# Two matmuls of 512 and 256 columns in place of three of 256 in a split-float32 network

## Chip, cores and metric

One Trainium2 chip, one core, one launch. The metric is the device time of the launch in microseconds (us); the time before is 1345.1 us, the median of three runs. A smaller time is better.

## What is computed

The reference takes 256 tokens of 1024 features through two blocks.

- Block 1: an RMS norm, one wide projection, sliding-window attention with 8 heads, chunkwise retention with 4 heads, two sigmoid gates that merge them, an output projection, and a SwiGLU feed-forward layer of 2816 hidden units.
- Block 2: a gated spatial mixer beside a banded attention, an output projection, and a PEER layer: a query projection per token, scores against two sets of 128 keys for each of 8 heads, a top-16 of the 16 x 16 sums of the best, and then, over the chosen ones of 16384 experts, `sum over experts of softmax(score) * gelu(u . x) * v`.

```python
u = jnp.take(expert_u, eidx, axis=0)
h = jax.nn.gelu(jnp.einsum('thkd,td->thk', u, xb))
vv = jnp.take(expert_v, eidx, axis=0)
return jnp.einsum('thk,thkd->td', (g * h.astype(jnp.float32)).astype(xb.dtype), vv)
```

The kernel computes the products with all experts densely and then multiplies by a matrix S of gates that is zero where an expert was not chosen.

## The kernel before

**Split products.** Every large product runs in `fp32r` with both factors split into a high and a low part, x = xh + xl and W = Wh + Wl, and keeps three of the four partial products. `mm3` (L105 to L109) issues them for one chunk of 128 along the contracted axis: Wh with xh (L107), Wh with xl (L108), Wl with xh (L109). The weights are the stationary operand (128 x 128), the activations stream with 256 columns, one per token, and all three add into the same 256 columns of a PSUM bank. `new_acts` (L206) keeps xh and xl in two tiles, `acth` and `actl` (also `hidh`, `atth`, `xbh`).

**Weights.** `unit_` (L80 to L97) loads a unit of up to 8 such chunks (512 KB) by one DMA on SP's queue into `raw` (4 buffers); ScalarE (ACT) copies it to `whi` (L94) and VectorE (DVE) subtracts to `wlo` (L95). The parts live in two pools of three buffers in the two blocks (`wa`, `wb`, taken in turn) and in `wb` alone in the PEER layer. A unit is asked for with a priority that lies 80 ahead (`AHEAD`), and the compiler's scheduler fixes from the priorities one order of instructions for each engine; every engine then works through its own in order.

**PSUM.** Eight banks of 512 columns: four named `mm`, handed out by `mm_bank` (L99) for these products, and four named `ax` (L102) for the rest.

**Who reads the banks.** A tile of 256 columns is read once, by the instruction that also uses it: the first projections by DVE with the norm's factor R (L286), the gates by DVE (L324), the att/ret pairs by DVE (L341, L342), `w_out`, `w_down` and `w_out2` by a DVE add of the residual (L357, L402, L645), the gated half of block 2 by DVE (L589), the queries by ACT (L898). In the feed-forward layer (gate and up) and in PEER's first layer (`first_layer`, L921) two units fill the two halves of one bank, which is read with 512 columns at once: DVE L383, and ACT's Gelu L933, L936.

**Order of the PEER layer.** Six queries with activations before the norm (`RAWQ`), then 128 units `peer_u`; among the first of them the other ten queries are laid in (after every third unit), with their score matmuls (L837), and DVE's top-k steps are handed out by a budget (`pump`). When those are done, two or three calls of `combine` (L851: four tokens each, DVE and ACT build one-hot matrices, 8 small matmuls) follow each pair of units. After that come 128 units `peer_v`, the second layer (L974), with 512 columns. `gemm_n` (L136), which makes some projections with the weights streaming in 512 columns, and the second layer use four or more banks directly.

Of the kernel before, what the change touches and what calls it, by code (L numbers as in the profile page):

```python
# [13 lines left out]
OP = mybir.AluOpType  # L14
# [28 lines left out]
class Net:  # L43
    def __init__(self, tc, a, out, stack):
        self.tc, self.nc, self.a, self.out, self.stack = tc, tc.nc, a, out, stack
        nc = self.nc
        self.const = self.pool("const", 1)
        self.psum = self.pool("psum", 1, space=PSUM)
        self.tiny = self.pool("tiny", 2)
        self.small = self.const.tile([128, NSMALL], F32, name="small")  # L50
# [47 lines left out]

    def mm_bank(self):  # L99
        return self.psum.tile([128, 512], F32, name="mm", bufs=4)  # L100
# [21 lines left out]
    def gemm_k(self, ps, parts, hl, ks, first=False, last=False):  # L122
        hi, lo = parts
        for k in ks:
            s = slice(k * 128, k * 128 + 128)
            self.mm3(ps, (hi[:, s], lo[:, s]), self.acts(hl, k), first and k == ks[0], last and k == ks[-1])

    def gemm_t_late(self, jobs, hl):
        """gemm_t of several (ps, src), with the last k after all others."""
# [6 lines left out]
    def gemm_n(self, src, hl):  # L136
        """two banks, one per 128 tokens, of [t, 512] for a chunk of 512 columns."""
# [19 lines left out]
    def rsqrt(self, y, ss, n, scale, pool=None):  # L157
        """y = (ss * scale + eps)^-1/2, all [128, n]."""
# [22 lines left out]
    def token_sums(self, acc):  # L181
        """[128 t, 2] from [128 d, 256 t] summed over d."""
# [6 lines left out]
    def rows(self, r, name):  # L189
        """[128, 256] with r of token t in column t, in every partition."""  # L190
# [40 lines left out]
    def block1(self, actp):  # L231
        nc, a, tc = self.nc, self.a, self.tc
        mult, add, sub = OP.mult, OP.add, OP.subtract
        with ExitStack():
# [19 lines left out]
            with ExitStack() as s1:  # L254
# [12 lines left out]
                for i, (dst, sc) in enumerate(dests):  # L267
                    ps = (self.ax_bank() if i in (3, 4) else self.mm_bank())[:, :T]
# [4 lines left out]
                    early.append((dst, sc, ps))  # L273
# [11 lines left out]
                    for d_, c_, p_ in early:  # L285
                        nc.vector.scalar_tensor_tensor(d_, p_, c_, R, op0=mult, op1=mult)  # L286
# [34 lines left out]
                for i in range(16):  # L321
                    ps = self.mm_bank()[:, :T]
                    self.gemm_t(ps, a["w_in_a"][14 + i], h, 8)
                    nc.vector.tensor_tensor(out=gate[:, i], in0=ps, in1=R, op=mult)  # L324
                    if i == 2:
                        self.turn_ret(osb, ret)
                    if i % 4 == 3:
                        g4 = gate[:, i - 3:i + 1].rearrange("p a b -> p (a b)")
                        nc.scalar.activation(g4, g4, AF.Sigmoid)
                mer = self.new_acts(actp)  # L330
                for m in range(8):
                    if m % 2 == 0:
                        hi, lo = self.unit(a["w_att_o"][m // 2], 1024)
                    ps = self.mm_bank()
                    for k in range(4):
                        s = slice((m % 2 * 4 + k) * 128, (m % 2 * 4 + k) * 128 + 128)
                        self.mm3(ps[:, :T], (hi[:, s], lo[:, s]), self.acts(att, k), k == 0, k == 3)
                    self.gemm_t(ps[:, T:], a["w_ret_o"][m], ret, 8)
                    m1 = p2.tile([128, T], F32, name="m1")
                    m2 = p2.tile([128, T], F32, name="m2")  # L340
                    nc.vector.tensor_tensor(out=m1, in0=ps[:, :T], in1=gate[:, m], op=mult)  # L341
                    nc.vector.tensor_tensor(out=m2, in0=ps[:, T:], in1=gate[:, 8 + m], op=mult)  # L342
                    nc.vector.tensor_tensor(out=m1, in0=m1, in1=m2, op=add)
# [4 lines left out]
                for m in range(8):  # L348
                    if m == 0:
                        two = [self.mm_bank()[:, :T] for _ in range(2)]  # L350
# [3 lines left out]
                    else:  # L354
                        ps = self.mm_bank()[:, :T]
                        self.gemm_t(ps, a["w_out"][m], mer, 8)
                    nc.vector.tensor_tensor(out=x1[:, m], in0=ps, in1=x0[:, m], op=add)  # L357
                    self.split(x1[:, m], h[0][:, m], h[1][:, m], self.col("norm_ffn", m))
                    self.accumulate_squares(acc, x1[:, m], m)
            with ExitStack() as s1:  # L360
# [4 lines left out]
                for f in range(KF):  # L365
                    ps = self.mm_bank()
                    if f == 0:
                        other = self.mm_bank()
                        self.gemm_t_late([(ps[:, :T], a["w_gate"][0]), (other[:, :T], a["w_up"][0])], h)
                        r = self.norm_column(acc, "rb")  # L370
                        early.append((ps[:, :T], other[:, :T]))
                        continue
                    self.gemm_t(ps[:, :T], a["w_gate"][f], h, 8)
                    if f == 2:
                        R = self.rows(r, "rb")
                    self.gemm_t(ps[:, T:], a["w_up"][f], h, 8)
                    early.append((ps.rearrange("p (a t) -> p a t", a=2), None))
                    if f == 1:
                        continue
                    for f0, (g, u) in enumerate(early, f + 1 - len(early)):  # L380
                        gu = p2.tile([128, 2, T], F32, name="gu")
                        if f0:
                            nc.vector.tensor_tensor(out=gu, in0=g, in1=R[:, None, :].to_broadcast([128, 2, T]),  # L383
                                                    op=mult)
                        else:
                            nc.vector.tensor_tensor(out=gu[:, 0], in0=g, in1=R, op=mult)
                            nc.vector.tensor_tensor(out=gu[:, 1], in0=u, in1=R, op=mult)
# [10 lines left out]
                for m in range(8):  # L398
                    ps = self.mm_bank()[:, :T]
# [114 lines left out]
    def block2(self, actp, x2, h, acc, acg):  # L514
        nc, a = self.nc, self.a
        mult, add, sub = OP.mult, OP.add, OP.subtract
        with ExitStack() as s1:
# [68 lines left out]
            def gated(m):  # L586
                ps = self.mm_bank()[:, :T]
                self.gemm_t(ps, a["w_in2_a"][m], h, 8)
                nc.vector.tensor_tensor(out=u[:, m], in0=ps, in1=R, op=mult)  # L589
# [30 lines left out]
            def begin(m):  # L620
                outs.append((self.mm_bank()[:, :T], self.unit(a["w_out2"][m], 1024)))
# [15 lines left out]
            for m in range(8):  # L637
# [4 lines left out]
                else:  # L642
                    ps = self.mm_bank()[:, :T]
                    self.gemm_t(ps, a["w_out2"][m], ab, 8)
                nc.vector.tensor_tensor(out=x3[:, m], in0=ps, in1=y, op=add)  # L645
# [56 lines left out]
    def peer(self, st, x3, h, acc):  # L702
# [181 lines left out]
        def query(c):  # L884
            nonlocal last, keys, r, R
            if c == 0:
                firsts[:] = [self.mm_bank()[:, :T] for _ in range(2)]
# [3 lines left out]
            else:  # L891
                ps = self.mm_bank()[:, :T]
# [5 lines left out]
            nc.scalar.activation(qT, ps, AF.Copy)  # L898
# [22 lines left out]
        def first_layer(j):  # L921
            nonlocal pair
            e = j % 2
            if e == 0:
                pair = self.mm_bank()
            self.gemm_t(pair[:, e * T:e * T + T], a["peer_u"][j], xb, 8)
# [3 lines left out]
            p3 = pair.rearrange("p (e t) -> p e t", e=2)  # L930
            if done:
                gt = cp.tile([128, 2, T], F32, name="gt", bufs=2)
                nc.scalar.activation(gt[:, :, :done], p3[:, :, :done], AF.Gelu_apprx_tanh)  # L933
                nc.vector.tensor_tensor(out=S[:, js, :done], in0=S[:, js, :done], in1=gt[:, :, :done], op=mult)
            if done < T:
                nc.scalar.activation(S[:, js, done:], p3[:, :, done:], AF.Gelu_apprx_tanh)  # L936
# [64 lines left out]
def wt(w, ks=None):  # L1001
    """[n chunk][128 k][k chunk * 128 n]"""
# [4 lines left out]
def wn(w):  # L1007
    """[n chunk of 512][pair of k chunks][128 k][2 * 512 n]"""
# [77 lines left out]
```

## Time and profile before

| | |
|---|---|
| three runs | 1344.84, 1345.1, 1346.21 us |
| profiled execution: span from first to last instruction | 1343.6 us |
| TensorE matmul (PE) busy | 1334.3 us, 99% |
| weight loads (PEld) busy, beside the matmuls | 1245.0 us, 93% |
| DVE busy | 935.0 us, 70% |
| ACT busy | 768.4 us, 57% |
| mean granted TensorE clock | 0.997 of full |

The profiled execution has no time of its own beside its span; the median is 1.5 us above that span. Durations below are from this execution. Matmuls overlap, so a matmul's own duration (some 0.28 us) says little; the interval from one start to the next says what it costs. "Issue interval" below means that interval.

### The profile page before, as it was taken

The numbers are of one execution on the slowest core, as the hardware profiler recorded it, in microseconds if no ns is written. First come the engines' busy times: TensorE is split into PE (matmuls) and PEld (weight loads), VectorE is DVE, ScalarE is ACT, GpSimd is POOL, SyncE is SP. The second block draws the span as 40 slices with busy tenths as digits, with TensorE's granted clock in tenths as the row PEclk, the third lists the DMA queues.
The fourth block names the chain that finished last, engine by engine and source line by source line (L and its number), as shares of the span: only waits on it lengthen the run. The fifth ranks groups of instructions, "written<-read, shape, count | busy, mean of one in ns | idle before, by whom it ended". The sixth has DMA issues, their size and how long they took to land.

```text
span 1343.6 us, 24086 instructions
## 1 busy us (share of the span) xinstructions
PE 1334.3 (99%) x9384; PEld 1245.0 (93%) x9384; DVE 935.0 (70%) x1826; ACT 768.4 (57%) x1306; POOL 9.7 (1%) x12
## 2 busy tenths in 40 slices
PE   8999999999999999999999999999999999999998
PEld 8878999999998899999999999999998888888887
DVE  6767576766666977966996667777656666665665
ACT  5456445544455766444458887776555555555553
POOL 2000000000000000000000000000000000000000
PEclk8999999999999999999999999999999999999999
DMA  8545666666566446656564444444576666666664
GB/s 267 179 137 159 187 179 185 186 189 181 176 192 228 142 138 181 191 180 184 151 197 147 142 141 137 140 137 139 157 219 190 192 198 191 194 195 191 196 194 126
DMA packets 67633, 236.27 MB, mean 176 GB/s; under 512 B 7616, under 2 KB 9536, under 8 KB 67392
## 3 DMA queue, kind: packets, MB, share of 16 engines
q1 hardware_dynamic: 66512, 233.14, 57.1%
q8 instruction: 73, 1.20, 0.4%
q10 hardware_dynamic: 1008, 1.61, 0.3%
q14 instruction: 40, 0.33, 0.1%
HBM read 232.62 MB, written 2.10 MB: 175 GB/s over the span
## 4 chain that ended last, share of the span: by engine, by line
PE 95%; DVE 2%; DMA 1%; issue 0%; ACT 0%; POOL 0%; SPq 0%; ACTq 0%; POOLq 0%; DVEq 0%
PE ax L974 26%; PE mm L107 21%; PE mm L109 21%; PE mm L108 21%; PE ax L872 5%; DVE wlo L95 1%; DMA raw<-in_w_in_a_dram 1%; PE ax L837 0%; DMA xT<-in_xT_dram 0%; ACT whi L94 0%; PE ax L663 0%; PE ax L698 0%; PE ax L464 0%; PE ax L452 0%; PE ax L685 0%
## 5 line engine op out<-in xcount | busy, mean ns | idle before, releaser
L95 DVE TENSOR_TENSOR wlo<-raw,whi 128x1024 fp32r<-128x1024 f32 (+2 forms) x433 | 524.5, 1213 | 225.9 <-ACT whi L94 224.8
L94 ACT ACTIVATE whi<-raw 128x1024 fp32r<-128x1024 f32 (+3 forms) x439 | 458.0, 1046 | 332.9 <-PE mm L108 249.0
L107 PE MATMUL mm<-xbh,whi 128*128 128x256 f32 x1104 | 316.2, 287 | 0.0
L109 PE MATMUL mm<-xbh,wlo 128*128 128x256 f32 x1104 | 312.4, 283 | 0.8 <-DVE wlo L95 0.7
L108 PE MATMUL mm<-xbl,whi 128*128 128x256 f32 x1104 | 312.1, 283 | 0.0
L107 PE MATMUL mm<-acth,whi 128*128 128x256 f32 x848 | 241.0, 284 | 1.7 <-ACT acth L248 1.0
L108 PE MATMUL mm<-actl,whi 128*128 128x256 f32 x848 | 239.7, 283 | 0.7 <-DVE actl L249 0.7
L109 PE MATMUL mm<-acth,wlo 128*128 128x256 f32 x848 | 239.6, 283 | 0.0
L109 PEld LDWEIGHTS mm<-xbh,wlo 128*128 128x128 f32 x1104 | 210.6, 191 | 1.3 <-DVE wlo L95 1.2
L107 PEld LDWEIGHTS mm<-xbh,whi 128*128 128x128 f32 x1104 | 211.2, 191 | 0.2
L108 PEld LDWEIGHTS mm<-xbl,whi 128*128 128x128 f32 x1104 | 210.8, 191 | 0.0
L107 PEld LDWEIGHTS mm<-acth,whi 128*128 128x128 f32 x848 | 161.3, 190 | 2.8 <-ACT acth L248 1.2
L108 PEld LDWEIGHTS mm<-actl,whi 128*128 128x128 f32 x848 | 161.2, 190 | 1.6 <-DVE actl L249 1.6
L109 PEld LDWEIGHTS mm<-acth,wlo 128*128 128x128 f32 x848 | 161.3, 190 | 0.2 <-DVE wlo L95 0.2
L974 PE MATMUL ax<-wlo,keys 128*128 128x512 f32 x512 | 158.0, 389 | 0.0
L974 PE MATMUL ax<-whi,q 128*128 128x512 f32 x512 | 158.0, 389 | 0.0
L974 PE MATMUL ax<-whi,keys 128*128 128x512 f32 x512 | 157.9, 389 | 0.0
L151 ACT ACTIVATE keys<-S 128x256 fp32r<-128x256 f32 x128 | 53.4, 418 | 151.5 <-PE ax L974 151.5
L974 PEld LDWEIGHTS ax<-whi,q 128*128 128x128 f32 x512 | 96.1, 188 | 20.0
L974 PEld LDWEIGHTS ax<-wlo,keys 128*128 128x128 f32 x512 | 96.1, 188 | 19.9
L974 PEld LDWEIGHTS ax<-whi,keys 128*128 128x128 f32 x512 | 96.1, 188 | 19.8
L865 ACT ACTIVATE G<-B,ga 128x128 f16<-128x128 f16 x256 | 98.0, 575 | 0.0
(277 smaller groups left out, 1468.7 us busy)
## 6 DMA issues: line engine op xcount, KB each, us to landing
raw<-in_peer_u_dram SPq DMA_DIRECT2D x128, 512.0 KB, 3.6
raw<-in_peer_v_dram SPq DMA_DIRECT2D x128, 512.0 KB, 4.2
raw<-in_w_in_b_dram SPq DMA_DIRECT2D x32, 512.0 KB, 4.3
raw<-in_w_in_a_dram SPq DMA_DIRECT2D x31, 512.0 KB, 3.9
raw<-in_w_gate_dram SPq DMA_DIRECT2D x22, 512.0 KB, 3.6
raw<-in_w_up_dram SPq DMA_DIRECT2D x22, 512.0 KB, 3.7
raw<-in_w_out_dram SPq DMA_DIRECT2D x16, 512.0 KB, 4.3
raw<-in_w_down_dram SPq DMA_DIRECT2D x16, 512.0 KB, 3.6
```

The costliest lines, as they stand in the source:

```text
L94: self.last_copy = nc.scalar.activation(hi[:, s], raw[:, s], AF.Copy).ins
L95: (engine or nc.vector).tensor_tensor(out=lo[:, s], in0=raw[:, s], in1=hi[:, s].bitcast(F32), op=OP.subtract)
L107: mm(ps, lhsT=left[0], rhs=right[0], start=first, stop=False)
L108: mm(ps, lhsT=left[0], rhs=right[1], start=False, stop=False)
L109: mm(ps, lhsT=left[1], rhs=right[0], start=False, stop=last)
L151: nc.scalar.activation(hi, src, AF.Copy)
L865: nc.scalar.activation(G[0][:, :, t], B[:, :, t], AF.Copy, scale=ga[:, t0 + t:t0 + t + 1])
L872: nc.tensor.matmul(C[:, t * 128:t * 128 + 128], lhsT=A[:, :, t], rhs=G[i][:, :, t], start=i == 0, stop=i == 1)
L974: nc.tensor.matmul(banks[tb][d], lhsT=s[left][:, ts], rhs=w[right][:, d * 512:d * 512 + 512], start=first, stop=end)
```

## The change

The activations' two parts become two halves of one tile of 512 columns for each chunk. A new `wide` issues one matmul of Wh with all 512 columns, into a whole bank (xh's product in the first half, xl's in the second), and one of Wl with xh's 256 columns into the first half. So one weight load and one matmul in three go, and the columns streamed stay the same (768). The bank's halves are added when it is read: `total` does it with an ACT copy of the second half to SBUF and a DVE add of the first; `plus` with two DVE adds.

A tile of 256 results now takes a whole bank. `mm_pair` makes tiles of two banks, two buffers; `mm_bank` hands out first one half of such a pair, then the other. What was one bank for two units (feed-forward, att/ret, first layer) is a pair. What used the bank on reading (the factor R, the gate, Gelu) now follows from SBUF as an instruction of its own. `gemm_n` and the second layer keep their matmuls. Docstrings were taken out.

```diff
+    def mm_pair(self):
+        return self.psum.tile([128, 2, 512], F32, name="mm", bufs=2)
     def mm_bank(self):
-        return self.psum.tile([128, 512], F32, name="mm", bufs=4)
+        if self.half is None:
+            self.half = self.mm_pair()
+            return self.half[:, 0]
+        pair, self.half = self.half, None
+        return pair[:, 1]
...
+    def wide(self, ps, w, hl, k, first, last):
+        mm = self.nc.tensor.matmul
+        mm(ps, lhsT=w[0], rhs=hl[2][:, k].rearrange("p h t -> p (h t)"), start=first, stop=False)
+        mm(ps[:, :T], lhsT=w[1], rhs=hl[0][:, k], start=False, stop=last)
+    def total(self, out, ps):
+        self.nc.scalar.activation(out, ps[..., T:], AF.Copy)
+        self.nc.vector.tensor_tensor(out=out, in0=ps[..., :T], in1=out, op=OP.add)
+    def plus(self, out, x, ps):
+        tt = self.nc.vector.tensor_tensor
+        tt(out=out, in0=ps[:, :T], in1=x, op=OP.add)
+        tt(out=out, in0=ps[:, T:], in1=out, op=OP.add)
...
-            self.mm3(ps, (hi[:, s], lo[:, s]), self.acts(hl, k0 + k),
-                     first and k == 0, last and k == K - 1)
+            self.wide(ps, (hi[:, s], lo[:, s]), hl, k0 + k, first and k == 0, last and k == K - 1)
...
     def new_acts(self, pool, K=8, tag="act", bufs=2):
-        return (pool.tile([128, K, T], F32R, tag=tag + "h", name=tag + "h", bufs=bufs),
-                pool.tile([128, K, T], F32R, tag=tag + "l", name=tag + "l", bufs=bufs))
+        both = pool.tile([128, K, 2, T], F32R, tag=tag, name=tag, bufs=bufs)
+        return both[:, :, 0], both[:, :, 1], both
...
-                    ps = self.mm_bank()[:, :T]
+                    ps = self.mm_bank()
                     self.gemm_t(ps, a["w_in_a"][14 + i], h, 8)
-                    nc.vector.tensor_tensor(out=gate[:, i], in0=ps, in1=R, op=mult)
+                    self.total(gate[:, i], ps)
...
-                        g4 = gate[:, i - 3:i + 1].rearrange("p a b -> p (a b)")
+                        g4 = gate[:, i - 3:i + 1]
+                        nc.vector.tensor_tensor(out=g4, in0=g4, in1=R[:, None, :].to_broadcast([128, 4, T]), op=mult)
                         nc.scalar.activation(g4, g4, AF.Sigmoid)
...
-                    nc.vector.tensor_tensor(out=x2[:, m], in0=ps, in1=x1[:, m], op=add)
+                    self.plus(x2[:, m], x1[:, m], ps)
...
-            nc.scalar.activation(qT, ps, AF.Copy)
+            self.total(qT, ps)
...
             if e == 0:
-                pair = self.mm_bank()
-            self.gemm_t(pair[:, e * T:e * T + T], a["peer_u"][j], xb, 8)
+                pair = self.mm_pair()
+            self.gemm_t(pair[:, e], a["peer_u"][j], xb, 8)
...
             if done:
                 gt = cp.tile([128, 2, T], F32, name="gt", bufs=2)
-                nc.scalar.activation(gt[:, :, :done], p3[:, :, :done], AF.Gelu_apprx_tanh)
+                self.total(gt, pair)
+                nc.scalar.activation(gt[:, :, :done], gt[:, :, :done], AF.Gelu_apprx_tanh)
                 nc.vector.tensor_tensor(out=S[:, js, :done], in0=S[:, js, :done], in1=gt[:, :, :done], op=mult)
+            else:
+                gt = S[:, js]
+                self.total(gt, pair)
             if done < T:
-                nc.scalar.activation(S[:, js, done:], p3[:, :, done:], AF.Gelu_apprx_tanh)
+                nc.scalar.activation(S[:, js, done:], gt[:, :, done:], AF.Gelu_apprx_tanh)
```

The scheduler's new order, at three places. In the changed kernel `unit_`'s two lines are L95 and L96, `wide` is L125 and L126, `total` L129 and L130, `plus` L135 and L136. A row is one instruction: line, operation, output and inputs with tile numbers, shape, and the semaphores it waits on (`DVE_49` counts DVE's instructions, `Activation_49` ACT's, `PE_49` TensorE's).

First place, TensorE in `w_down`, at the change from one output tile to the next (`hid` is the hidden activations, `whi` and `wlo` the unit's parts, `mm` the bank). Before:

```order
L107 MATMUL mm_4171<-hidh_2474,whi_4233 128x256
L108 MATMUL mm_4171<-hidl_2475,whi_4233 128x256
L109 MATMUL mm_4171<-hidh_2474,wlo_4234 128x256
L107 MATMUL mm_4265<-hidh_2474,whi_4267 128x256 [waits Activation_49]
L108 MATMUL mm_4265<-hidl_2475,whi_4267 128x256
L109 MATMUL mm_4265<-hidh_2474,wlo_4268 128x256 [waits DVE_49]
```

Now:

```order
L126 MATMUL mm_3444<-hid_2102,wlo_3491 128x256
L125 MATMUL mm_3589<-hid_2102,whi_3591 128x512 [waits DVE_49,Activation_49]
L126 MATMUL mm_3589<-hid_2102,wlo_3592 128x256 [waits DVE_49]
L125 MATMUL mm_3589<-hid_2102,whi_3591 128x512
L126 MATMUL mm_3589<-hid_2102,wlo_3592 128x256
L125 MATMUL mm_3589<-hid_2102,whi_3591 128x512
L126 MATMUL mm_3589<-hid_2102,wlo_3592 128x256
L125 MATMUL mm_3589<-hid_2102,whi_3591 128x512
L125 MATMUL mm_3444<-hid_2102,whi_3518 128x512 [waits DVE_49]
L126 MATMUL mm_3444<-hid_2102,wlo_3519 128x256
```

Before, the next tile (`mm_4265`) follows at once and its two waits are for its weights. Now the first tile of pair `mm_3444` ends, seven matmuls of another pair follow, and the first matmul of the second half of `mm_3444` waits for DVE's two adds (L135, L136) that read its first half.

Second place, TensorE in the PEER layer where queries are laid in (`xb` the normed activations, L861 the score matmuls, `qT` a query read from its bank, `mm_5288` and `mm_5311` two pairs of the two buffers, `mm_5387` the pair that takes the buffer of `mm_5288`):

```order
L125 MATMUL mm_5288<-xb_4915,whi_5356 128x512
L126 MATMUL mm_5288<-xb_4915,wlo_5357 128x256
L861 MATMUL ax_5467<-keys_5334,qT_5336 128x128 [waits DMAHW5_49,DVE_49]
L861 MATMUL ax_5467<-keys_5334,qT_5336 128x128
L125 MATMUL mm_5311<-xb_4915,whi_5443 128x512 [waits Activation_49]
L126 MATMUL mm_5311<-xb_4915,wlo_5444 128x256 [waits DVE_49]
L125 MATMUL mm_5311<-xb_4915,whi_5443 128x512
L126 MATMUL mm_5311<-xb_4915,wlo_5444 128x256
L125 MATMUL mm_5311<-xb_4915,whi_5443 128x512
L125 MATMUL mm_5387<-xb_4915,whi_5389 128x512 [waits DVE_49]
L126 MATMUL mm_5387<-xb_4915,wlo_5390 128x256
```

The last matmul of `mm_5288` is followed by two score matmuls and five of `mm_5311`; then `mm_5387` waits until DVE has read `mm_5288`.

Third place, DVE among the gates of block 1 (`gate<-mm` at L130 is the add of `total`):

```order
L96 TENSOR_TENSOR wlo_1431<-raw_1429,whi_1430 128x1024 [waits DMAHW0_49,PE_49,Activation_49]
L130 TENSOR_TENSOR gate_1091<-mm_1228,gate_1091 128x256 [waits Activation_49]
L96 TENSOR_TENSOR wlo_1404<-raw_1402,whi_1403 128x1024 [waits DMAHW7_49,Activation_49]
L130 TENSOR_TENSOR gate_1091<-mm_1277,gate_1091 128x256 [waits Activation_49]
L96 TENSOR_TENSOR wlo_1455<-raw_1453,whi_1454 128x1024 [waits DMAHW1_49,PE_49,Activation_49]
L130 TENSOR_TENSOR gate_1091<-mm_1277,gate_1091 128x256 [waits Activation_49]
```

Each add that reads a bank now stands behind a weight subtraction (`wlo`) which itself waits for ACT's `whi` and for TensorE to have done with an earlier unit.

## Rows read from the trace of the kernel before

**Rows 1.** Page, part 1 (busy time, share, instructions) and the granted clock by slices.

```profile
PE 1334.3 (99%) x9384; PEld 1245.0 (93%) x9384; DVE 935.0 (70%) x1826; ACT 768.4 (57%) x1306; POOL 9.7 (1%) x12
...
PEclk8999999999999999999999999999999999999999
```

**Rows 2.** Page, part 4, the chain that ended last, by engine and line.

```profile
PE 95%; DVE 2%; DMA 1%; issue 0%; ACT 0%; POOL 0%; SPq 0%; ACTq 0%; POOLq 0%; DVEq 0%
PE ax L974 26%; PE mm L107 21%; PE mm L109 21%; PE mm L108 21%; PE ax L872 5%; DVE wlo L95 1%; DMA raw<-in_w_in_a_dram 1%; PE ax L837 0%; DMA xT<-in_xT_dram 0%; ACT whi L94 0%; PE ax L663 0%; PE ax L698 0%; PE ax L464 0%; PE ax L452 0%; PE ax L685 0%
```

**Rows 3.** Groups by form, L107: tile and inputs, shape, count | busy us, mean ns.

```profile
L107 PE MATMUL mm<-xbh,whi 128*128 128x256 f32 x1104 | 316.2, 287 | 0.0
...
L107 PE MATMUL mm<-acth,whi 128*128 128x256 f32 x848 | 241.0, 284 | 1.7 <-ACT acth L248 1.0 <-DVE aq L286 0.7
...
L107 PE MATMUL mm<-hidh,whi 128*128 128x256 f32 x176 | 49.4, 281 | 0.0
```

**Rows 4.** PE timeline, 256 columns: PEER layer, then gates (start, duration; 18 and 33 intervals).

```profile
699.74 0.28 PE L107 MATMUL mm<-xbh,whi 128*128 128x256 f32 x1
...
701.90 0.28 PE L107 MATMUL mm<-xbh,whi 128*128 128x256 f32 x1
...
148.01 0.28 PE L107 MATMUL mm<-acth,whi 128*128 128x256 f32 x1
...
151.92 0.28 PE L107 MATMUL mm<-acth,whi 128*128 128x256 f32 x1
```

**Rows 5.** 512 columns: chain's row of the second layer; PE timeline of `gemm_n` (23 intervals).

```profile
991.45 347.52 PE ax L974 x1533
...
106.46 0.39 PE L108 MATMUL mm<-wlo,acth 128*128 128x512 f32 x1
...
111.83 0.39 PE L107 MATMUL mm<-whi,acth 128*128 128x512 f32 x1
```

**Rows 6.** PE, ACT and DVE timelines where one gate's unit ends at 150.50.

```profile
150.50 0.28 PE L107 MATMUL mm<-acth,whi 128*128 128x256 f32 x1
...
150.63 1.06 ACT L94 ACTIVATE whi<-raw 128x1024 fp32r<-128x1024 f32 x1 [1.78 <-PE mm L108]
...
150.70 0.42 DVE L324 TENSOR_TENSOR gate<-mm,ra 128x256 f32<-128x256 f32 x1 [0.60 <-PE mm L109]
151.72 1.23 DVE L95 TENSOR_TENSOR wlo<-raw,whi 128x1024 fp32r<-128x1024 f32 x1 [0.60 <-ACT whi L94]
```

**Rows 7.** DVE timeline in the combine stage, where an instruction follows `wlo` without a gap.

```profile
782.86 1.22 DVE L95 TENSOR_TENSOR wlo<-raw,whi 128x1024 fp32r<-128x1024 f32 x1
783.99 0.80 DVE L875 SCALAR_TENSOR_TENSOR S<-ax,S 128x280 f32<-128x280 f32 x2
```

**Rows 8.** Groups by form: reads of a bank by ACT and DVE; one-hot copies of `combine`.

```profile
L898 ACT ACTIVATE qT<-mm 128x256 f32<-128x256 f32 x16 | 5.9, 368 | 0.4 <-ACT xt L918 0.4
...
L936 ACT ACTIVATE S<-mm 128x512 f32<-128x512 f32 x26 | 15.1, 580 | 0.0
...
L383 DVE TENSOR_TENSOR gu<-mm,rb 128x512 f32<-128x512 f32 x21 | 14.5, 691 | 9.4 <-PE mm L109 9.3
...
L865 ACT ACTIVATE G<-B,ga 128x128 f16<-128x128 f16 x256 | 98.0, 575 | 0.0
```

**Rows 9.** Windows: length; busy us (instructions) of PE, PEld, DVE, ACT, POOL; clock, DMA share, GB/s.

```profile
654.00:699.00 45.00, 44.23 (x365) 43.69 (x364) 44.53 (x111) 22.98 (x29) 0.00 (x0) 1.00 0.54 159
705.00:958.00 253.00, 253.00 (x2119) 250.76 (x2118) 182.48 (x353) 192.30 (x453) 0.00 (x0) 1.00 0.47 141
```

**Rows 10.** DVE timeline of 654 to 699 (first and last `wlo`, 14 intervals), and PE's wait there.

```profile
654.09 1.21 DVE L95 TENSOR_TENSOR wlo<-raw,whi 128x1024 fp32r<-128x1024 f32 x1
...
698.64 2.35 DVE L95 TENSOR_TENSOR wlo<-raw,whi 128x1024 fp32r<-128x1024 f32 x2
...
PE mm L109 <- DVE wlo L95: 0.7, 1, 0.7
```

More of the change, by code (lines that the diff above doesn't have):

```diff
@@ L125, in gemm_k @@
             s = slice(k * 128, k * 128 + 128)
-            self.mm3(ps, (hi[:, s], lo[:, s]), self.acts(hl, k), first and k == ks[0], last and k == ks[-1])
+            self.wide(ps, (hi[:, s], lo[:, s]), hl, k, first and k == ks[0], last and k == ks[-1])
     def gemm_t_late(self, jobs, hl):
@@ L272, in block1 @@
                     self.gemm_t(ps, a["w_in_a"][i], h, 8, parts=parts, engine=nc.gpsimd if i in (4, 5) else None)
-                    early.append((dst, sc, ps))
+                    self.total(dst, ps)
+                    early.append((dst, sc))
                     if i == 1:
@@ L284, in block1 @@
                         R = self.rows(r, "ra")
[L285 to L286 removed]
+                    for d_, c_ in early:
+                        nc.vector.scalar_tensor_tensor(d_, d_, c_, R, op0=mult, op1=mult)
                     early = []
@@ L333, in block1 @@
                         hi, lo = self.unit(a["w_att_o"][m // 2], 1024)
-                    ps = self.mm_bank()
+                    ps = self.mm_pair()
                     for k in range(4):
                         s = slice((m % 2 * 4 + k) * 128, (m % 2 * 4 + k) * 128 + 128)
[L337 to L343, printed above, removed]
+                        self.wide(ps[:, 0], (hi[:, s], lo[:, s]), att, k, k == 0, k == 3)
+                    self.gemm_t(ps[:, 1], a["w_ret_o"][m], ret, 8)
+                    mm = p2.tile([128, 2, T], F32, name="mm")
+                    self.total(mm, ps)
+                    nc.vector.tensor_tensor(out=mm, in0=mm, in1=gate[:, m:m + 9:8], op=mult)
+                    m1 = mm[:, 0]
+                    nc.vector.tensor_tensor(out=m1, in0=m1, in1=mm[:, 1], op=add)
                     self.split(m1, mer[0][:, m], mer[1][:, m])
@@ L349, in block1 @@
                     if m == 0:
-                        two = [self.mm_bank()[:, :T] for _ in range(2)]
+                        two = [self.mm_bank() for _ in range(2)]
                         self.gemm_t_late(list(zip(two, a["w_out"][0:2])), mer)
@@ L354, in block1 @@
                     else:
-                        ps = self.mm_bank()[:, :T]
+                        ps = self.mm_bank()
                         self.gemm_t(ps, a["w_out"][m], mer, 8)
-                    nc.vector.tensor_tensor(out=x1[:, m], in0=ps, in1=x0[:, m], op=add)
+                    self.plus(x1[:, m], x0[:, m], ps)
                     self.split(x1[:, m], h[0][:, m], h[1][:, m], self.col("norm_ffn", m))
@@ L365, in block1 @@
                 for f in range(KF):
-                    ps = self.mm_bank()
+                    ps = self.mm_pair()
                     if f == 0:
-                        other = self.mm_bank()
-                        self.gemm_t_late([(ps[:, :T], a["w_gate"][0]), (other[:, :T], a["w_up"][0])], h)
+                        self.gemm_t_late([(ps[:, 0], a["w_gate"][0]), (ps[:, 1], a["w_up"][0])], h)
                         r = self.norm_column(acc, "rb")
-                        early.append((ps[:, :T], other[:, :T]))
-                        continue
[L373 to L387, printed above, removed]
+                    else:
+                        self.gemm_t(ps[:, 0], a["w_gate"][f], h, 8)
+                        if f == 2:
+                            R = self.rows(r, "rb")
+                        self.gemm_t(ps[:, 1], a["w_up"][f], h, 8)
+                    gu = p2.tile([128, 2, T], F32, name="gu", bufs=3)
+                    self.total(gu, ps)
+                    early.append((f, gu))
+                    if f < 2:
+                        continue
+                    for f0, gu in early:
+                        nc.vector.tensor_tensor(out=gu, in0=gu, in1=R[:, None, :].to_broadcast([128, 2, T]), op=mult)
                         nc.scalar.activation(gu[:, 0], gu[:, 0], AF.Silu)
@@ L642, in block2 @@
                 else:
-                    ps = self.mm_bank()[:, :T]
+                    ps = self.mm_bank()
                     self.gemm_t(ps, a["w_out2"][m], ab, 8)
-                nc.vector.tensor_tensor(out=x3[:, m], in0=ps, in1=y, op=add)
+                self.plus(x3[:, m], y, ps)
                 self.split(x3[:, m], h[0][:, m], h[1][:, m], self.col("ln_ffn", m))
@@ L886, in query @@
             if c == 0:
-                firsts[:] = [self.mm_bank()[:, :T] for _ in range(2)]
+                firsts[:] = [self.mm_bank() for _ in range(2)]
                 self.gemm_t_late(list(zip(firsts, a["w_q"][0:2])), h)
```

16 lines of the change are left out of this document (9 added, 7 removed).

## The prediction
> **What bounds the kernel now.** I read the busy times first: TensorE works 99% of the span, weight loads run beside it for 93%, VectorE (DVE) has 30% and ScalarE (ACT) 43% of the time free [rows 1]. The granted clock is at its full level, 2.4 GHz, in all slices but the first. The chain of waits agrees: 95% of it is TensorE, three times 21% of that the lines of `mm3` [rows 2]. So whatever shortens TensorE's own work shows in the time, and whatever makes TensorE wait shows as well. For other engines' work one asks only whether something waits for it.
>
> Then what a matmul costs. In the PEER layer 18 issue intervals of 256-column matmuls take 701.90 - 699.74 = 2.16 us, 120.0 ns each; among the gates 33 take 3.91 us, 118.5 ns [rows 4]. In the second layer 1533 matmuls of 512 columns take 347.52 us, 226.7 ns each; in `gemm_n` 23 intervals take 5.37 us, 233.5 ns [rows 5]. From 256 to 512 columns the price rises by 106.7 ns, not by 120: some 13 ns of a matmul with its weight load don't depend on the columns. Those 13 ns are what the change can save, once for each three.
>
> **Term 1, the dropped matmul.** A triple costs 360.0 ns in the PEER layer and would cost 226.7 + 120.0 = 346.7, a gain of 13.3; with 1104 triples there [rows 3] this is 14.7 us. In the blocks it is 355.5 against 226.7 + 118.5 = 345.2, a gain of 10.3; with 848 + 176 triples 10.5 us. Together **-25.2 us**. That is the good end as rows show it, since every row of either width pays for its load. At the other end the wide matmul costs what it does in `gemm_n`, 233.5: gains of 6.5 and 3.5 ns, so 7.2 + 3.6 = 10.8 us. I take 25.2, because the second layer's matmuls come in the same setting (PEER layer, weights from the same pool) and are by far the larger sample.
>
> **Term 2, reading the halves: added work on ACT and DVE.** A read of 256 columns costs ACT 368 ns and a read of 512 costs 580; DVE takes 691 for 512 [rows 8] and 0.42 us for 256 [rows 6]. Each tile or pair gains one ACT copy and one DVE instruction of that size, where one read was enough. As busy time I cost this at nothing, because ACT and DVE are 57% and 70% busy; the cover goes where DVE has no time left, which is term 4. What matters first is when the read is over, for the bank is free only then.
>
> **Term 3, the wait for a bank.** Before, four `mm` banks go round one by one, and waits for a bank's reader are all but absent (0.7 us behind L286 in the row of the 848 [rows 3]): a gate's unit ends at 150.50, and DVE reads it at 150.70, done at 151.12, 0.6 us after the end [rows 6]. DVE can do so since ACT makes the next `whi` meanwhile (150.63, 1.06 us), and `wlo` comes after (151.72).
>
> Now the read needs both engines in turn, and the order puts weights ahead of it on both. After the unit's end `whi` starts 0.13 later; 1.09 after that `wlo`; the next DVE instruction starts 1.13 after `wlo` [rows 7]; the add takes 0.42. The read ends **0.13 + 1.09 + 1.13 + 0.42 = 2.77 us after the unit's end**, call it the latency L. With `whi` alone ahead (0.13 + 1.06 + 0.37 + 0.42) it is near 1.95; with nothing ahead (0.13 + 0.37 + 0.06 + 0.42) near 1.0. Pairs and `plus` add 0.3.
>
> Whether TensorE waits depends on the work it has between the end of a tile and the instruction that needs the buffer: the cover. The order shows about 145 such waits. A stall is L less the cover, the cover being the matmuls in between by the intervals above:
>
> - Feed-forward gate and up, att/ret, PEER units after the queries: a whole other pair lies between, 16 x 346.7 ns = 5.5 us. No stall.
> - Gates: 12 of 17 waits have less, from 0.1 to 2.8 us, 1.9 on average: 10.7 us. `w_out`, 4 waits, 5.9 us. Block 2, 7 waits, 2.0 on average: 6.6 us.
> - `w_down`: seven matmuls of the other pair lie between, four wide and three narrow, 1.27 us. Two `wlo` stand ahead of DVE's adds, but their buffers were freed 12 or 13 matmuls before the unit's end, so L is only about 2.05 there. Four waits, 3.2 us.
> - First projections: the weights ahead wait for no earlier unit there, so I take 1.95: 5 waits, 2.5 us.
> - Query stage: a query's pair occupies one of the two buffers, so the first-layer pairs reuse the other. Cover 1.2 us (two score matmuls and five more) in the place that the order shows, 1.4 to 2.9 elsewhere: 17 waits, 17.7 us; before it, among the raw queries, 2.1 us.
>
> Sum **+48.7 us**. With L at 1.95 everywhere it would be 26, at 1.0 only 5, and with 2.77 everywhere 59. Among the queries a second `wlo` often stands ahead; were it always late, 17 x 1.13 = 19 us more. I take 48.7 because the order has `wlo` ahead of nearly every add, and the profile shows `whi` starting on the unit's end.
>
> **Term 4, DVE without slack.** From 654 to 699 us, where the last top-k steps run, DVE is busy 44.53 of 45 us [rows 9], `wlo` comes every 44.55 / 14 = 3.18 us, where a unit needs 24 x 0.120 = 2.88, and TensorE waits for one `wlo` [rows 10]. DVE sets the pace there. Seven more adds of 0.69 are 4.8 us, and 15 units' gain of term 1 (8 x 13.3 ns each, 1.6 us) can't be had: 6.4 at most, 0 at least. I take **+3**, since TensorE's stalls just before give the steps a head start.
>
> DMA traffic and SP's queue are as before; nothing moves past them but with the units themselves.
>
> **Sum.** -25.2 + 48.7 + 3 = +26.5 us on a profiled execution whose span is 1343.6, so 1370 us of span; the median of the runs is 1.5 us above the span. Forecast **1371 us**, slower.
>
> **The rivals.**
>
> - *B, faster: the reads keep up.* If the copy and the add are not held by `whi` and `wlo` (because the weights were made earlier, so the engines pass them by the time a tile ends), L is 1.0 to 1.2 and the stalls 5 to 8 us: 1345.1 - 25.2 + 5 + 2 = 1327 us. For it speak the idle 30% of DVE; against it that `whi` starts 0.13 us after the unit's end, released by TensorE [rows 6], so it isn't early. It decides from L below some 1.7 us.
> - *C, slower still: the combine stage.* There ACT is busy 192.3 of 253 us and DVE 182.5 [rows 9], and I count no loss. If the pair's copy waits behind eight one-hot copies of 575 ns [rows 8], L is 1.0 + 0.3 + 4.6 = 5.9 us and more than the cover of 5.5; 0.5 us for each of 38 pairs is 19 us: 1390 us.
> - *D, the dropped load was free.* The wide matmul costs more than the second layer's, by the lower end of term 1: 1345.1 - 10.8 + 48.7 + 3 = 1386 us. The Trainium skill, page "TensorE: Matmul & The Clock Gate", section "Wait — 56ns, not 53.3ns?", gives N / 2.4 GHz + about 2.5 ns between starts of warm matmuls; by that a triple would save only 2.5 ns, 5.3 us for 2128 triples, and the sum would be an estimated 1392 us. The trace doesn't agree: 13.3 ns at the full granted clock for both widths [rows 4, 5].
>
> **How the numbers follow.** My forecast has 0.78: L between 1.95 and 2.77 (with 19 us of second subtractions at the far end) and term 4 between 0 and 6.4. Its own range is 1345.1 - 25.2 + 26 = 1346 to 1345.1 - 25.2 + 59 + 19 + 6 = 1404 us. B has 0.14, C 0.05, D 0.03. A part of 0.05 at the low end of my own case falls within 0.2%, which is about what a measurement of this kernel tells from no change. So faster 0.14, same 0.05, slower 0.81. The range from 1338 to 1403 leaves out most of B and a little above: about 2 in 10.
>
> **What the changed profile would show.** Right: 512-column rows of `wide` at 227 ns, PE's busy share down to 95 or 96%, and rows of TensorE waiting for the adds of `total` and `plus`, over a dozen each in the gates and the query stage, of about 1 us, and none in gate and up or in the combine stage. Wrong in term 1: 512-column intervals of 234. Wrong in term 3: few such waits, with the copy starting some 0.1 us after a unit's end (B). Waits in the combine stage would speak for C. A lower granted clock after stalls, which I cost at nothing, would make it slower than my sum.

## The result: 1386.1 us, slower by 3%

The change runs in 1386.11 us (median of 4 runs, 1383.14 to 1389.47) where the kernel before takes 1345.1 beside it: a ratio of 1.0305, 95% interval 1.0281 to 1.033, 41.0 us more. (A fourth run of the kernel before, 1834.21 us, was in a slow state of the chip and is not counted.) The forecast was 1371 with a range of 1338 to 1403. The profiled execution spans 1385.8 us, 42.2 more than before.

Page of the changed kernel: busy times with the granted clock, and the chain's shares.

```profile
PE 1333.5 (96%) x7208; PEld 1131.4 (82%) x7208; DVE 1015.2 (73%) x1973; ACT 836.8 (60%) x1438; POOL 9.7 (1%) x12
...
PEclk9999999999999999999999999999999999999999
...
PE 83%; DVE 8%; ACT 4%; issue 3%; DMA 1%; POOL 0%; ACTq 0%; DVEq 0%; POOLq 0%
```

Against [rows 1, 2]: 2176 matmuls and loads fewer, DVE 80 us and ACT 68 us busier, TensorE's share of the chain down from 95 to 83%. The slices of the clock row are too coarse here: the mean granted clock is 0.991, before 0.997. Two first projections that used `ax` banks before take halves of pairs now.

TensorE's waits in the changed kernel (us in all, times, longest; L130 is the add of `total`, L136 the second of `plus`):

```profile
PE mm L125 <- DVE S L130: 8.1, 7, 2.0
PE mm L125 <- DVE gate L130: 7.2, 6, 2.2
PE mm L126 <- DVE wlo L96: 6.3, 6, 1.5
PE mm L125 <- DVE xT L136: 5.2, 5, 1.5
PE mm L125 <- DVE act L276: 4.7, 3, 2.4
PE mm L125 <- DVE aq L130: 3.0, 2, 2.5
PE mm L125 <- ACT whi L95: 2.5, 4, 0.6
PE ax L861 <- DVE qT L130: 2.4, 2, 1.9
PE mm L125 <- ACT v L640: 2.1, 1, 2.1
PE mm L125 <- DVE qT L130: 1.6, 2, 1.2
```

Before, from 500 to 720 us, one wait of 0.7 us for a `wlo` was all [rows 10]. The waits for a bank's read are there, in the gates, the residual adds (`xT`), `gemm_n`'s banks (`v`), and the first-layer pairs (`S`) and queries (`qT`) that alternate. With three small ones (`rq`, `rk`, `u`) they sum to 28.3 us in 26. Another 8.8 us are waits for weights (`wlo`, `whi`).

Where the time went is read from TensorE's timeline: each chunk of the contracted axis ends with one narrow matmul of the low weights (L109 before, L126 now), 2176 of them, in nearly the same order. The table gives the start of the n-th of them before, and how much later it starts in the change and in five of the experiments below (us, each from the two timelines).

| n | up to | before | change | e1 | e2 | e3 | e4 | e5 |
|---|---|---|---|---|---|---|---|---|
| 240 | gates | 164.6 | +11.1 | +9.5 | +10.8 | -0.5 | +6.1 | +1.2 |
| 400 | `w_out` | 221.6 | +15.0 | +12.5 | +14.7 | -1.8 | +9.3 | +1.3 |
| 752 | gate and up | 347.8 | +11.5 | +11.0 | +11.2 | -5.1 | +5.8 | +1.5 |
| 928 | `w_down` | 410.5 | +11.4 | +12.3 | +11.1 | -6.7 | +5.8 | +1.5 |
| 1072 | block 2, raw queries | 525.7 | +26.3 | +19.3 | +21.0 | -6.3 | +16.8 | +3.0 |
| 1392 | queries among pairs | 645.5 | +46.6 | +43.0 | +18.2 | -9.3 | +34.7 | +3.0 |
| 1536 | last top-k steps | 700.0 | +48.7 | +47.2 | +18.9 | -8.6 | +36.8 | +5.6 |
| 2175 | combine stage, end | 990.8 | +42.2 | +47.3 | +12.1 | -14.5 | +30.4 | +5.6 |

The change loses up to the gates, in block 2 and among the queries, and gains where a whole pair covers each read: 3.5 us over gate and up, 6.5 us in the combine stage.

One wait in full, of the changed kernel's timeline (first-layer pairs with a query between; start, duration):

```profile
579.22 0.40 PE L125 MATMUL mm<-xb,whi 128*128 128x512 f32 x1
579.23 1.06 ACT L95 ACTIVATE whi<-raw 128x1024 fp32r<-128x1024 f32 x1 [1.71 <-PE mm L125]
...
579.41 0.87 DVE L746 MAX8 stop<-sc 128x8 f32<-128x128 f32 x4
...
580.20 0.58 ACT L129 ACTIVATE S<-mm 128x512 f32<-128x512 f32 x1
...
581.03 0.29 DVE L748 FIND_INDEX8 itop<-stop,sc 128x8 uint32<-128x128 f32 x1
...
581.24 1.22 DVE L96 TENSOR_TENSOR wlo<-raw,whi 128x1024 fp32r<-128x1024 f32 x1
...
582.36 0.69 DVE L130 TENSOR_TENSOR S<-mm,S 128x512 f32<-128x512 f32 x1
...
583.11 0.50 PE L125 MATMUL mm<-xb,whi 128*128 128x512 f32 x1 [1.99 <-DVE S L130]
```

A pair ends at 579.2. ACT first makes the next `whi`, then copies; DVE is still in top-k steps (L746, L748), then does `wlo`, then the add, which ends at 583.05. That is a latency of 3.8 us. TensorE has five chunks of another tile to do meanwhile, 1.9 us, and stands still for 1.99.

### The profile page after: what moved, and what is told of

Its sections match the earlier page's. It is cut to its first block, busy times and chain, and to the rows that moved or that the text cites. A ratio compares the mean times of both kernels' runs of the same rounds, so it can differ in the third digit from the quotient of the medians.

```text
span 1385.8 us, 20023 instructions
## 1 busy us (share of the span) xinstructions
PE 1333.5 (96%) x7208; PEld 1131.4 (82%) x7208; DVE 1015.2 (73%) x1973; ACT 836.8 (60%) x1438; POOL 9.7 (1%) x12
## 4 chain that ended last, share of the span: by engine, by line
PE 83%; DVE 8%; ACT 4%; issue 3%; DMA 1%; POOL 0%; ACTq 0%; DVEq 0%; POOLq 0%
PE mm L125 31%; PE ax L1001 25%; PE mm L126 15%; PE ax L896 4%; DVE wlo L96 4%; ACT whi L95 2%; PE mm L117 2%; PE mm L119 2%; PE mm L118 2%; DMA raw<-in_w_in_a_dram 1%; DVE S L130 1%; DVE itop L748 1%; ACT s L698 1%; DVE stop L746 0%; PE ax L722 0%
## 5 line engine op out<-in xcount | busy, mean ns | idle before, releaser
L96 DVE TENSOR_TENSOR wlo<-raw,whi 128x1024 fp32r<-128x1024 f32 (+2 forms) x433 | 524.7, 1213 | 222.9 <-ACT whi L95 217.3
L95 ACT ACTIVATE whi<-raw 128x1024 fp32r<-128x1024 f32 (+3 forms) x439 | 458.3, 1047 | 280.2 <-PE mm L125 166.1
L125 PE MATMUL mm<-xb,whi 128*128 128x512 f32 x1104 | 396.7, 401 | 12.5 <-DVE S L130 8.1
L125 PE MATMUL mm<-act,whi 128*128 128x512 f32 x864 | 310.1, 401 | 23.5 <-DVE gate L130 5.9
L126 PE MATMUL mm<-xb,wlo 128*128 128x256 f32 x1104 | 310.5, 282 | 6.3 <-DVE wlo L96 6.3
L125 PEld LDWEIGHTS mm<-xb,whi 128*128 128x128 f32 x1104 | 208.6, 189 | 62.2 <-DVE S L130 10.7
L126 PE MATMUL mm<-act,wlo 128*128 128x256 f32 x864 | 241.3, 282 | 0.0
L125 PEld LDWEIGHTS mm<-act,whi 128*128 128x128 f32 x864 | 163.6, 190 | 66.9 <-DVE gate L130 7.8
L126 PEld LDWEIGHTS mm<-xb,wlo 128*128 128x128 f32 x1104 | 209.7, 190 | 8.5 <-DVE wlo L96 8.2
L126 PEld LDWEIGHTS mm<-act,wlo 128*128 128x128 f32 x864 | 164.7, 191 | 1.2
L896 PE MATMUL ax<-G,A 128*128 128x128 f16 x512 | 66.6, 296 | 0.0
L125 PE MATMUL mm<-hid,whi 128*128 128x512 f32 x176 | 61.3, 393 | 0.0
```

Of the source, the lines that this page charges most:

```text
L95: self.last_copy = nc.scalar.activation(hi[:, s], raw[:, s], AF.Copy).ins
L96: (engine or nc.vector).tensor_tensor(out=lo[:, s], in0=raw[:, s], in1=hi[:, s].bitcast(F32), op=OP.subtract)
L125: mm(ps, lhsT=w[0], rhs=hl[2][:, k].rearrange("p h t -> p (h t)"), start=first, stop=False)
L126: mm(ps[:, :T], lhsT=w[1], rhs=hl[0][:, k], start=False, stop=last)
L896: nc.tensor.matmul(C[:, t * 128:t * 128 + 128], lhsT=A[:, :, t], rhs=G[i][:, :, t], start=i == 0, stop=i == 1)
```

## The experiments

Theory A: TensorE waits for banks, because a read needs ACT and DVE in turn behind the weights' parts, and tiles of two banks leave little other work meanwhile. Theory B: the added copies and adds fill ACT and DVE. Theory C: what costs is a low clock after pauses. Theory D: the dropped matmul saved nothing. An edit also changes the scheduler's order on each engine; no run holds that order fixed.

**e1, three matmuls again, all else as in the change.**

```diff
-        mm(ps, lhsT=w[0], rhs=hl[2][:, k].rearrange("p h t -> p (h t)"), start=first, stop=False)
+        mm(ps[:, :T], lhsT=w[0], rhs=hl[0][:, k], start=first, stop=False)
+        mm(ps[:, T:], lhsT=w[0], rhs=hl[1][:, k], start=False, stop=False)
```

> As the change, but each chunk again takes three matmuls of 256 columns (high weights with the high activations into the first half of the bank, high with low into the second, low with high into the first). The buffers and the reads stay as in the change. Theory A (TensorE waits for banks that are read late, and the dropped matmul saves some 25 us): the gain is lost and the waits stay, a little shorter as the cover grows: 1386 + 25 less 2 to 6 for the longer cover, 1405 to 1409 us. Theory D (the dropped matmul saves nothing): 1386 us. Theory B (the added copies and adds fill ACT and DVE, and the weights come late): these engines pace the kernel, so longer matmuls matter little: 1386 to 1392 us.

One run: 1392.63 us, 6.5 more than the change, where A said 19 to 23 and D nothing. The table says where. In gate and up, `w_down` and the combine stage, where nothing waits for a read, e1 falls 10.0 us behind the change (2.0, 1.4 and 6.6). Up to the end of `w_out`, where reads are waited for, it is 2.4 us ahead: there a longer matmul mainly shortens the waits (15.2 us of them against 20.1 in the change), while my number let the gain stand everywhere. In block 2 it is 7.9 us ahead; there the clock stays at its full level in e1 and not in the change (more below), which hides much of the rest. By itself this run can't tell A from B; e3 does.

**e2, the queries in the other banks.**

```diff
-                firsts[:] = [self.mm_bank() for _ in range(2)]
+                firsts[:] = [self.ax_bank() for _ in range(2)]
...
-                ps = self.mm_bank()
+                ps = self.ax_bank()
```

> As the change, but the queries go to the other four banks (ax) instead of to halves of the pairs, so that in the stage where queries and first-layer pairs alternate both pair buffers serve the first layer. Work and instructions are the same. Theory A: the waits for a pair's read in that stage lose most of the 25 us that this stage costs more than before; 1360 to 1370 us. Theory B (DVE and ACT are too busy in that stage): nothing changes there, 1384 to 1388 us. Theory C (the low clock after long stalls is what costs): as A where the stalls go, the two stretches of low clock in this stage go too; without the stalls' end it stays.

1358.55 us, ratio to before 1.0116 (1.0095 to 1.0137): 27.6 us less than the change and a little below A's range. From chunk 1072 to 1392 the change loses 20.3 us; e2 gains 2.8. The work on DVE is the same, so B falls for this stage. TensorE's waits there shrink from 15.6 us to 0.5, those for weights among them.

**e3, four tiles of one bank.**

```diff
     def mm_pair(self):
-        return self.psum.tile([128, 2, 512], F32, name="mm", bufs=2)
+        return [self.mm_bank(), self.mm_bank()]
     def mm_bank(self):
...
+        return self.psum.tile([128, 512], F32, name="mm", bufs=4)
...
     def total(self, out, ps):
+        if isinstance(ps, list):
+            for i in range(2):
+                self.total(out[:, i], ps[i])
+            return
```

> As the change, but mm is four tiles of one bank again instead of two tiles of two, each released by its own read; a pair is two such tiles, read by two copies and two adds of 256 columns instead of one each of 512 (more time on ACT and DVE: 2 x 0.37 for 0.58, 2 x 0.42 for 0.69 us). Theory A: four buffers of one bank give three other tiles as cover, 2 to 8 us, so nearly no wait for a read is left: 1345.7 - 25 + 0 to 10, 1321 to 1331 us. Theory B: more work on DVE and ACT, so as slow as the change or slower, 1386 to 1400 us.

1331.9 us, ratio 0.9922 (0.9898 to 0.9945): faster than both kernels and just above A's range. DVE and ACT are busier than in the change, so B falls altogether. Page, part 1:

```profile
PE 1314.7 (99%) x7208; PEld 1125.7 (85%) x7208; DVE 1018.8 (77%) x2067; ACT 841.1 (63%) x1530; POOL 9.7 (1%) x12
```

And its list of TensorE's waits, those above 1 us, none of them for the read of a bank of `mm`:

```profile
PE mm L119 <- DVE act L274: 3.1, 2, 2.2
PE ax L818 <- DVE pick L812: 1.5, 1, 1.5
PE ax L220 <- ACT dg L219: 1.4, 1, 1.4
PE ax L59 <- DVE ones L54: 1.1, 1, 1.1
```

**e4, the gates read by DVE alone,** in the change.

```diff
+        self.nc.vector.tensor_copy(out, ps[..., T:])
+        self.nc.vector.tensor_tensor(out=out, in0=ps[..., :T], in1=out, op=OP.add)
```

> As the change, but the 16 gates of block 1 are read by DVE alone (a DVE copy of the second half, then the add) so that the read doesn't queue behind ACT's weight copy. Theory A: the read ends 1.0 to 2.2 us after the unit's end instead of 2.8 (a weight subtraction still stands between in places), and of the 8 us that the gates lose against before 3 to 8 come back: 1378 to 1383 us, and nothing else changes. Theory B: DVE gets 16 x 0.42 us more work and the time stays or grows: 1386 to 1390 us.

One run: 1375.73 us, 10.4 less, below A's range. Up to the gates' end 5.0 us come back, as A said; another 6.3 us come back in block 2 and among the queries, which the edit doesn't touch. TensorE's waits in these two stages are the same, 23.4 us here and 23.9 in the change; the clock is not. Block 2 with the raw queries, first in the change, then here (columns as in [rows 9]):

```profile
421.80:551.90 130.10, 121.79 (x684) 99.85 (x684) 99.72 (x246) 84.51 (x158) 1.04 (x2) 0.95 0.47 158
416.20:542.40 126.20, 118.13 (x684) 97.12 (x683) 98.00 (x238) 83.79 (x157) 1.04 (x2) 0.99 0.49 161
```

The waits of the gates shrink from 7.2 us in 6 to 1.2 in 1:

```profile
PE mm L125 <- DVE gate L134: 1.2, 1, 1.2
```

**e5, three matmuls with four single banks:** the edit of e1 on e3.

> As the run with four single banks, but each chunk takes three matmuls of 256 columns into the two halves, so that the dropped matmul is priced where hardly anything waits for a bank. Theory A: combine stage and feed-forward lose the full 13.3 and 10.3 ns per triple, and only the places where DVE paces the run with four banks (it shows 14.5 us gained of the 25.2) hide some: 1331.9 + 15 to 25, 1347 to 1357 us. Theory D (the dropped matmul is free): 1332 us.

1349.34 us, ratio 1.0038 (1.0025 to 1.0052): 17.4 us more than e3, as A said, and D falls. By the two ratios to the kernel before it is 15.6 us; in the traces the 2176 chunks take 20.1 us longer than in e3, 9.2 ns each. Against before, e5 has the change's reads and none of its saving: +4.1 us by the medians is what the reads cost when they hold no bank.

**e6 and e7, the 16 gates on one bank and on two,** in e3.

```diff
+                held = [self.mm_bank() for _ in range(1)]
                 for i in range(16):
-                    ps = self.mm_bank()
+                    ps = held[i % 1]
```

e7 has 2 in both places of the 1.

> As the run with four single banks, but the 16 gates of block 1 share one bank, so that the cover between two gates is nothing and TensorE's pause between them shows the latency of the read itself. Theory A: a pause of about 2.8 us (weight copy 1.06, weight subtraction 1.2, add 0.42) before each of 15 gates, 42 us: 1374 us. If the copy and the add were not held by the weights: pauses of 0.8 to 1.2 us, 12 to 18 us, 1344 to 1350 us.

One run: 1375.99 us, A's 1374. Two gates of its timeline:

```profile
150.88 0.38 ACT L127 ACTIVATE gate<-mm 128x256 f32<-128x256 f32 x1 [2.24 <-PE mm L120]
...
151.29 0.42 DVE L128 TENSOR_TENSOR gate<-mm,gate 128x256 f32<-128x256 f32 x1 [3.75 <-ACT gate L127]
151.78 0.50 PE L119 MATMUL mm<-act,whi 128*128 128x512 f32 x1 [0.93 <-DVE gate L128]
...
154.78 1.06 ACT L95 ACTIVATE whi<-raw 128x1024 fp32r<-128x1024 f32 x1 [2.58 <-issue]
155.75 0.36 ACT L127 ACTIVATE gate<-mm 128x256 f32<-128x256 f32 x1
155.87 1.22 DVE L96 TENSOR_TENSOR wlo<-raw,whi 128x1024 fp32r<-128x1024 f32 x1 [2.40 <-ACT whi L95]
157.01 0.42 DVE L128 TENSOR_TENSOR gate<-mm,gate 128x256 f32<-128x256 f32 x1
157.49 0.50 PE L119 MATMUL mm<-act,whi 128*128 128x512 f32 x1 [2.67 <-DVE gate L128]
```

The first read comes ahead of the weights, and TensorE pauses for 0.93 us; the second stands behind `whi` and `wlo`, and the pause is 2.67 us. That is the latency by itself, forecast at 1.0 and 2.77. The waits for the gates sum to 23.5 us in 11, not A's 42. Much of the rest of the 44 us is the clock, in the window of the gates (columns as in [rows 9]):

```profile
125.00:195.00 70.00, 45.17 (x180) 35.91 (x178) 22.29 (x32) 19.44 (x31) 0.00 (x0) 0.80 0.27 89
```

At 0.80 of the full clock 14 of these 70 us are lost cycles, some of them in pauses, where they cost nothing. So the total agreed with A partly by chance.

> As the run with four single banks, but the 16 gates of block 1 go round two banks, so that the cover is one gate, 8 x 345 ns = 2.76 us, about the latency of the read. Theory A: pauses of 0 to 0.4 us for each gate, 0 to 5 us, 1332 to 1337 us. Theory B (work of ACT and DVE counts, not the wait): 1332 us here and in the run with one bank.

One run: 1332.88 us, one wait of 0.4 us at a gate. Two banks are enough if each is a tile of its own. The change has four halves in two tiles and loses 7 us at the gates: not the number of banks decides, but that a half waits for its neighbour's read.

```profile
PE mm L119 <- DVE gate L128: 0.4, 1, 0.4
```

**e8, e3 with the queries in the other banks** (the edit of e2).

> As the run with four single banks, and the queries in the ax banks. Theory A: with four banks no wait for a read was left in the query stage, and what holds that stage is DVE; so nothing is gained, 1330 to 1334 us. If waits for banks were still there: 1324 to 1329 us.

1333.68 us, ratio 0.9923 (0.9903 to 0.9944): nothing gained over e3. The banks are no longer what holds the query stage.

**e9, e3 with some low parts made by GpSimd.**

```diff
-            self.gemm_t(pair[e], a["peer_u"][j], xb, 8)
+            self.gemm_t(pair[e], a["peer_u"][j], xb, 8, engine=nc.gpsimd if not ready and j % 4 == 1 else None)
```

> As the run with four single banks, but while the top-k steps run GpSimd makes every fourth first-layer unit's low part (some nine units) instead of DVE. If DVE sets the pace there (busy 105.23 of 115 us and then 39.86 of 40 in the run with four banks, where 448 triples gained 2.2 us of the 6.0 that the dropped matmul would save), 9 x 1.22 = 11 us of its work go and 2 to 5 us come back: 1327 to 1330 us. If something else holds that stage: 1331 to 1333 us. If GpSimd's 2.4 us per unit come late, or slow DVE down: 1333 to 1345 us.

1343.37 us, ratio 0.999 (0.998 to 1.0001), 11.5 more than e3: the third of the cases. Between chunks 1088 and 1408 the gain is 2.0 us with less work on DVE and 2.1 in e3, so DVE doesn't hold that stretch. Most of the loss comes behind it, where the last top-k steps run and GpSimd made more units than I had counted (13 more than in e3, 15 in all), each 2.5 us. One `wlo` of DVE now came 3.8 us late. The clock takes part too: it falls to the lower level during that wait (from 666 to 673 us) and at two other places, from 523 and from 690 us, for some 14 us together, so up to 7 us of the loss are lost cycles; e3 has none there. The group of GpSimd's subtractions, a line of TensorE's waits, and the window of the late `wlo`:

```profile
L96 POOL TENSOR_TENSOR wlo<-raw,whi 128x1024 fp32r<-128x1024 f32 x15 | 37.2, 2481 | 267.8 <-ACT whi L95 230.6 <-DVE oh L803 27.1 <-DVE oh L807 10.1
```

```profile
PE mm L120 <- DVE wlo L96: 4.0, 2, 3.8
```

```profile
666.00:674.00 8.00, 6.30 (x22) 5.44 (x23) 7.90 (x16) 3.66 (x6) 0.23 (x1) 0.57 0.48 161
```

## Why the prediction was right, and where its sizes were off

Forecast +26, measured +41.0 by the medians. The direction and the kind of mechanism (term 3) hold: e2, e3 and e7 take the wait away in three ways, and the loss goes with it; e6 shows the latency itself. The sizes don't: term 3's waits for reads are 28.3 us in the trace and not 48.7, and losses that the sum lacked made up for it, so that the total came nearer than its terms. The sign that I gave, over a dozen such waits each in the gates and the query stage, came out as 6 each.

By stage, from the table and the terms: up to the gates forecast +10.7 (2.5 + 10.7 of waits less 240 chunks at 10.3 ns), measured +11.1. `w_out` with att/ret +4.3, measured +3.9. Gate and up -3.6, measured -3.5. `w_down` +1.4, measured -0.1. Block 2 with the raw queries +7.2, measured +14.9. The query stage +13.4, measured +20.3. The last top-k steps +1.1, measured +2.1. The combine stage -8.5, measured -6.5. So two stages hold most of the miss.

**A step that failed: the clock at full level throughout, "which I cost at nothing".** Windows of the changed kernel (columns as in [rows 9]):

```profile
490.00:500.00 10.00, 8.43 (x38) 6.11 (x39) 5.96 (x7) 6.48 (x11) 0.00 (x0) 0.66 0.80 262
545.00:553.00 8.00, 6.45 (x23) 5.24 (x24) 8.00 (x30) 3.30 (x9) 0.00 (x0) 0.62 0.48 150
577.00:584.00 7.00, 5.01 (x30) 4.17 (x29) 7.00 (x27) 4.03 (x6) 0.00 (x0) 1.00 0.27 90
584.00:589.00 5.00, 5.00 (x22) 4.30 (x21) 3.42 (x22) 1.06 (x1) 0.00 (x0) 0.66 0.59 190
```

Three times TensorE stands still for about 2 us (2.07 for `v`, 1.92 for a query, the 1.99 shown above), and within 1.5 us of its end the clock falls to the lower level, 1.2 GHz. Not every such pause does that: 2.46 us among the first projections and 2.21 at a gate were followed by full clock. A wide matmul's start is then 0.64 us from the next wide one's instead of 0.35:

```profile
549.58 0.63 PE L125 MATMUL mm<-act,whi 128*128 128x512 f32 x1
...
550.22 0.63 PE L125 MATMUL mm<-act,whi 128*128 128x512 f32 x1
```

The cycles lost are 0.34 x 10 + 0.38 x 8 + 0.34 x 5 = 8.1 us; some fall into pauses. e4, with the same waits and one such stretch instead of three, is 6.3 us faster in block 2 and the query stage, which is about the price of the other two. The change's four runs agree: those with a mean clock of 0.990 and 0.991 took 1389.47 and 1387.59 us, those with 0.995 and 0.996 took 1383.14 and 1384.62. In block 2 with the raw queries the waits of all kinds sum to 8.3 us, near the forecast (8.7), and the clock is most of the miss. Theory C is thus a part of A, not a rival: e2 has fewer pauses and keeps the clock through the whole query stage, and e3 has none of these stretches.

**The other: in the query stage I counted reads alone.** The latency was right: of the pair reads that TensorE waits for there, the one of 3.8 us shown above, with top-k steps ahead of `wlo`, is an exception; the three that end at 611.7, 638.8 and 666.2 us took 3.05, forecast 3.07. In the first of them the pair ends at 608.6 and the add at 611.66:

```profile
608.74 1.06 ACT L95 ACTIVATE whi<-raw 128x1024 fp32r<-128x1024 f32 x1 [1.77 <-PE mm L125]
...
610.98 0.68 DVE L130 TENSOR_TENSOR S<-mm,S 128x512 f32<-128x512 f32 x1
...
611.71 0.50 PE L125 MATMUL mm<-xb,whi 128*128 128x512 f32 x1 [1.06 <-DVE S L130]
```

But only six waits for reads are there, 7.0 us, where I had 17 and 17.7 us. Nine more, 8.1 us, are for the parts of weights, which I had at nothing; for example

```profile
602.16 0.39 PE L126 MATMUL mm<-xb,wlo 128*128 128x256 f32 x1 [1.04 <-DVE wlo L96]
```

With 0.5 us for a query's scores that makes 15.6 us. Each wait costs more than its row says: from start to start the one of 1.06 us loses 1.22, and the wide matmul behind it is 0.34 us ahead of its narrow one instead of 0.23. For 16 waits that is an estimated 4 us; the low clock and the smaller term 1 add to it. Why the weights come late isn't settled: e2 and e3 lose these waits together with those for reads, so they go with the shared pairs and not with the work, but no run takes away one kind alone.

**Term 1 was 16 to 20 us, not 25.2** (e5 against e3). The wide matmul costs 347 ns with its narrow one in places, as forecast, and more in others. Changed kernel, a unit pair before and one after `combine`'s matmuls, 10 and 11 chunks apart:

```profile
801.75 0.39 PE L125 MATMUL mm<-xb,whi 128*128 128x512 f32 x1
...
805.22 0.39 PE L125 MATMUL mm<-xb,whi 128*128 128x512 f32 x1
...
807.82 0.40 PE L125 MATMUL mm<-xb,whi 128*128 128x512 f32 x1
...
811.71 0.40 PE L125 MATMUL mm<-xb,whi 128*128 128x512 f32 x1
```

That is 347.0 and 353.6 ns for a chunk. What makes the second slower isn't settled; the mean gain of e5's traces, 9.2 ns, lies between what `gemm_n`'s 233.5 ns [rows 5] gives and what the second layer's row gives, which I took. Besides, there are 2176 triples; I counted 2128.

**Rivals.** B (reads that keep up) is not what happened here; e3, where hardly a read holds TensorE, shows about the time that it would have given, 1332 where B said 1327. C (the combine stage loses) is wrong: no wait for a read there, 6.5 us gained. D's 1386 us is the measured time, but by luck: e5 shows 16 to 20 us saved where D has 10.8, and the low clock and the waits for weights, which the runs show, are not in D's sum. The Trainium skill's 2.5 ns ("TensorE: Matmul & The Clock Gate", "Wait — 56ns, not 53.3ns?") would save an estimated 5.3 us, which e5 doesn't bear out either.

## What to carry to other kernels

A saving on the bounding engine counts in full only in stages where that engine doesn't wait; where it waits for a result to be read out, most of it can come back as a longer wait (e1 against the change, up to `w_out`). So before merging output buffers, compare for each reuse the latency of the read, with all that stands ahead of it on each engine's queue, with the work that lies between: here 2.7 us against 1.2 to 2.8. Keep the buffers as separate tiles, so that each is released by its own read: that edit (e3) turned a loss of 3.0% into a gain of 0.8%. And where a read and the next weights share an engine's queue, count late weights as well as late reads.

## What the runs showed that was not expected

- Three pauses of about 2 us were each followed by the lower clock; between its start and its end the kernel before had no such stretch.
- In e6 the same happened at the gates, where TensorE stands still again and again for 2.7 us: up to 14 us of lost cycles beside 23 us of waits.
- The first wide matmul after a matmul of another type (scores, `combine`) starts its narrow one 0.32 us later instead of 0.23, and before the change a 256-column one 0.20 instead of 0.12: some 0.09 us for each such switch, in both kernels alike. After a pause without such a switch it is about the same (0.34 for 0.23).
